# The gate product of an encoder layer by Strassen's seven products, with low parts and norm sums moved to POOL

## The chip, the cores and the metric

The kernel runs on one core of one Trainium2 chip. The metric is the device time of one execution in microseconds (us). The engines are called as the profile calls them: PE (matrix products; PEld is its weight load), DVE (vector), ACT (activations and scaled copies), POOL (the general-purpose engine, which also issues DMAs that add into their target) and SP (the queue that issues plain DMAs). Each engine takes its instructions in order, from a queue of its own; semaphores tie the queues together.

## The reference

The reference is one layer of a causal encoder on 1024 positions of width 1024, in float32. Ahead of what is changed here come a pooling mixer, chunked attention, an output projection and a gated MLP of width 2816, whose last product adds into the residual `h`. The change concerns what follows:

```python
hn = rmsnorm(h, norm_ple_g[i])
gate = jax.nn.sigmoid(hn @ w_ple_gate[i] + b_ple_gate[i])   # 1024 x 1024 x 1024
h = h + gate * (p[i] @ w_ple[i])                            # 1024 x 256 x 1024
return rmsnorm(h, final_g)
```

## The kernel before

Everything is kept transposed: `H[d]` (d = 0 to 7) holds 128 features of the residual on the partitions, and the 1024 positions in the free dimension, in two halves `HS[0]` and `HS[1]` of 512. Float32 products are made of three matmuls (`mm3`, lines 135 to 137): each operand is split into a high part, rounded by a copy on ACT (line 140), and a low part, the rest, subtracted on DVE (line 141); the three are high by high, high by low, low by high. They add up in PSUM, whose eight banks of 128 x 512 are `PS[:, 0]` to `PS[:, 7]`.

The body of the kernel (the MLP) is the same before and after. The end of the kernel, which is rebuilt, has these stages, in the order in which PE takes them (PE's order is that of the code; the orders of DVE, ACT, POOL and SP are set by a scheduler, from priorities in the order of the code and its own estimate of when things are ready):

- *PLE product, first half* (`ple_mm(0, d, ...)`): `p @ w_ple` for positions 0 to 511, 8 tiles of 6 matmuls, copied by ACT to `po` (line 1314).
- *Last down tiles, first half* (`down_mm(d, 0, ...)`): the last two of the MLP's 22 row blocks, 8 tiles of 6 matmuls; DVE adds each into `H[d]` (line 1071). Between them stand the 8 tiles of the PLE product's second half.
- *Last down tiles, second half* (`down_mm(d, 1, ...)`): 8 tiles again.
- *Gate product*: 8 output tiles for the first half (`gate_mm`), 8 for the second, of which the last three are cut into 256 positions each. A tile of 512 positions takes 8 x 3 matmuls. The weights `w_gate` come in 8 loads of 512 KB, are split on ACT and DVE, and stay resident.
- After each tile `gate_out` (lines 1348 to 1352): multiply by the norm's factors in `rst2` (first half only; for the second half the operand was normed beforehand, `normed2`), sigmoid on ACT, times `po`, added to `H[d]`.
- *End*: the last norm, transposes on PE (`turn`), a scaled copy, and the store.

A norm (class `Norm`) has these steps: ACT squares each `H[d]` (lines 809, 811), DVE adds the squares (line 813), PE sums over the partitions (`sums`, line 819), DVE scales the sums (line 822), POOL raises them to the power -1/2 (line 823), PE spreads the result over the partitions (`rows`, line 827), ACT copies it out (line 829). `norm_a` and `norm_b` are the two halves' norms ahead of the gate; `last` are those of the end, whose `emit` (line 1367) multiplies the finished `H` and stores it. `sums` and `rows` are on PE's in-order queue: for `norm_a` they stood after the first and after the second gate tile.

Of the kernel before, what the change touches and what calls it, by code (L numbers as in the profile page):

```python
# [6 lines left out]
F32 = mybir.dt.float32  # L7
# [4 lines left out]
P = 128  # L12
SEQ = 1024
# [87 lines left out]
def trunk(tc, xT, pT, vecs, w_qk0, w_in, w_v, bias, counts, pool_w, w_out, w_up, w_down,  # L101
# [4 lines left out]
    with tc.tile_pool(name="sb", bufs=1) as sb, \  # L106
# [5 lines left out]
        R = sb.tile([P, 32768], F32R, name="R")  # L112
# [3 lines left out]

        b_pool = tc.tile_pool(name="b1", bufs=1)
# [4 lines left out]
        def r(kb, n):  # L122
            if kb >= 128:
                return B[:, int((kb - 128) * KW):int((kb - 128) * KW) + n]
            return R[:, int(kb * KW):int(kb * KW) + n]

# [31 lines left out]
        xh = [r(32 * h, 8192) for h in range(2)]  # L158
        XTH = [a[:, 0:4096].rearrange("p (k t) -> p k t", k=KT) for a in xh]
        XTL = [a[:, 4096:8192].rearrange("p (k t) -> p k t", k=KT) for a in xh]  # L160
        V = r(64, 8192).rearrange("p (k h c) -> p k h c", k=NTOK, h=N_HEADS)
# [104 lines left out]
        def v_outs(t, half, ps):  # L266
# [3 lines left out]
            hi, lo = V[:, t, hs, 0:HD], V[:, t, hs, HD:2 * HD]  # L270
# [172 lines left out]
        def values(u):  # L443
# [23 lines left out]
            for j in range(2):  # L467
                for n_, (part, k) in enumerate(todo):
                    a, b = reach[k]
                    b0 = block_at(k, a)  # L470
                    pe.matmul(Os[j][:, (a - t0) * P:(b - t0) * P].rearrange("p (t q) -> p t q", q=P), V[:, k, 2 * c_ + j],  # L471
# [799 lines left out]
        b_pool.__exit__(None, None, None)  # L1271
        b_pool = tc.tile_pool(name="po", bufs=1)
        PO = b_pool.__enter__().tile([P, 7168], F32, name="PO")
        po = [PO[:, 512 * n:512 * (n + 1)] for n in range(14)] + [V[:, 0:512], V[:, 512:1024]]
        for d in range(4):
# [3 lines left out]
        wg = [(r(b, 1024), r(b + 4, 1024)) for b in (16, 24, 80, 88, 44, 52)] + [(r(b, 1024), r(b + 8, 1024)) for b in (96, 112)]  # L1279
        hp = [[(r(b, 512), r(b + 2, 512)) for b in bs]  # L1280
              for bs in ((100, 108, 116, 124, 32, 36, 40, 60), (0, 4, 8, 12, 64, 68, 72, 76))]
        rawg = [f(44, 1024), f(48, 1024), f(52.25, 1024)]
        ng = [0]

        def gate_weights(ks):
            for k in ks:
                t = rawg[ng[0] % 3]
                ng[0] += 1
                sp.dma_start(t, w_gate[k])
                split(t, *wg[k])  # L1290

        rst2 = f(48.25, SEQ)
        norm_a = Norm(HS[0], f(56.25, 512), [f(58.25, 512)], 5, 1)
        norm_b = Norm(HS[1], f(52.25, 512), [f(54.25, 512)], 4, 1)

        def weighted2(h, k, src=None):
            hi, lo = hp[h][k]
            src, g = H[k][:, HS[h]] if src is None else src, vec[:, C_GP + k:C_GP + k + 1]
            act.activation(hi, src, AF.Copy, scale=g)
            dve.scalar_tensor_tensor(lo, src, g, rv(hi), ALU.mult, ALU.subtract)  # L1300

        def normed2(k):

            t = f(44 + 2 * (k % 2), 512)
            dve.tensor_tensor(t, H[k][:, HS[1]], rst2[:, HS[1]], ALU.mult)
            weighted2(1, k, t)

        ple_banks = (0, 1, 2, 4, 5, 6, 7, 3)
# [6 lines left out]

        for d in range(KT):
# [9 lines left out]
        for k in range(KT):  # L1326
            weighted2(0, k)
        gate_weights(range(4, 8))
# [178 lines left out]
```

## Time and profile before

| | |
|---|---|
| median of 3 runs | 1124.37 us (1124.28 to 1124.96) |
| profiled execution, its own time | 1124.14 us |
| its span, first to last instruction | 1122.3 us (1.8 us lie around it) |
| mean granted PE clock | 0.998 |
| PE busy in the end stages, 976.6 to 1113.0 us of the span | all of it |
| busy from 1020.2 to 1113.0 us (the gate) | PE 92.8, DVE 58.2, ACT 43.6, POOL 4.3 us |
| from the gate's last matmul to the end | 9.3 us |

The page gives each engine's busy time; a busy PE counts overlapping matmuls once, so the distance between two matmuls' starts says what one costs. In a row of the timeline stand start, duration, engine, line, operation and tiles, and in brackets the idle time before it and what ended that. A group row of the lines view has busy time and mean duration (ns) of one instruction.

### The profile page before, as it was taken

The numbers are of one execution on the slowest core, as the hardware profiler recorded it, in microseconds if no ns is written. First come the engines' busy times: TensorE is split into PE (matmuls) and PEld (weight loads), VectorE is DVE, ScalarE is ACT, GpSimd is POOL, SyncE is SP. The second block draws the span as 40 slices with busy tenths as digits, with TensorE's granted clock in tenths as the row PEclk, the third lists the DMA queues.
The fourth block names the chain that finished last, engine by engine and source line by source line (L and its number), as shares of the span: only waits on it lengthen the run. The fifth ranks groups of instructions, "written<-read, shape, count | busy, mean of one in ns | idle before, by whom it ended". The sixth has DMA issues, their size and how long they took to land.

```text
span 1122.3 us, 16025 instructions
## 1 busy us (share of the span) xinstructions
PE 1112.2 (99%) x5866; PEld 932.0 (83%) x5866; DVE 853.5 (76%) x1442; ACT 583.7 (52%) x1010; POOL 166.7 (15%) x212
## 2 busy tenths in 40 slices
PE   9999999999999999999999999999999999999997
PEld 7978799888888888888888888888888888888887
DVE  7466676678668878878787878787877789986845
ACT  8366676665664544444443435343444444664634
POOL 0012000186003200210122011201120112000000
PEclk9999999999999999999999999999999999999999
DMA  8101020204610352674667455756575556430003
GB/s 282 38 20 62 20 63 19 61 19 132 196 35 5 99 161 87 159 170 133 159 152 171 138 160 142 175 144 155 144 170 151 132 154 132 147 94 20 1 26 124
DMA packets 64591, 124.86 MB, mean 111 GB/s; under 512 B 7296, under 2 KB 8704, under 8 KB 64512
## 3 DMA queue, kind: packets, MB, share of 16 engines
q1 hardware_dynamic: 50400, 98.33, 27.0%
q0 software_dynamic: 13824, 25.17, 14.0%
q8 instruction: 46, 0.75, 0.3%
q10 hardware_dynamic: 288, 0.33, 0.1%
q14 instruction: 33, 0.27, 0.1%
HBM read 109.13 MB, written 14.68 MB: 110 GB/s over the span
## 4 chain that ended last, share of the span: by engine, by line
PE 89%; DVE 4%; issue 3%; ACT 2%; POOL 1%; DMA 0%; POOLq 0%; SPq 0%; DVEq 0%; ACTq 0%
PE PS L135 28%; PE PS L136 28%; PE PS L137 27%; PE PS L471 2%; PE PS L396 2%; PE PS L419 1%; DVE R L141 1%; DVE B L439 1%; ACT F L376 1%; ACT R L140 1%; DMA F<-in_xT 0%; POOL TB L966 0%; PE PS L819 0%; DVE F L948 0%; DVE F L1232 0%
## 5 line engine op out<-in xcount | busy, mean ns | idle before, releaser
L135 PE MATMUL PS<-R 128*128 128x512 f32 (+1 forms) x1152 | 441.2, 383 | 0.1
L137 PE MATMUL PS<-R 128*128 128x512 f32 (+1 forms) x1152 | 437.2, 380 | 0.0
L136 PE MATMUL PS<-R 128*128 128x512 f32 (+1 forms) x1088 | 419.3, 385 | 0.3 <-DVE R L245 0.3
L135 PEld LDWEIGHTS PS<-R 128*128 128x128 f32 x1152 | 216.9, 188 | 45.0 <-issue 2.5
L137 PEld LDWEIGHTS PS<-R 128*128 128x128 f32 x1152 | 216.8, 188 | 40.9
L136 PEld LDWEIGHTS PS<-R 128*128 128x128 f32 x1088 | 204.7, 188 | 40.5 <-DVE R L245 1.1
L140 ACT ACTIVATE R<-F 128x512 fp32r<-128x512 f32 (+2 forms) x221 | 137.3, 636 | 176.4 <-PE PS L136 77.1
L141 DVE TENSOR_TENSOR R<-F,R 128x512 fp32r<-128x512 f32 (+2 forms) x221 | 154.2, 712 | 49.3 <-ACT R L140 48.8
L891 DVE TENSOR_TENSOR F<-F 128x512 f32<-128x512 f32 x88 | 60.5, 688 | 49.5 <-DMA F<-in_w_up 45.9
L1201 DVE TENSOR_TENSOR F<-F,PS 128x512 f32<-128x512 f32 x140 | 92.5, 682 | 5.9 <-PE PS L137 5.8
L140 ACT ACTIVATE BQ<-RW 128x512 fp32r<-128x512 f32 x90 | 52.6, 622 | 78.6 <-PE PS L136 74.6
L1144 POOL DMA_DIRECT2D RW<-Yd x56 | 49.2, 879 | 266.9 <-DMA RW<-Yd 202.8
L1144 POOL DMA_DIRECT2D RW<-in_w_down x40 | 36.1, 951 | 225.0 <-DMA RW<-in_w_down 190.6
L141 DVE TENSOR_TENSOR BQ<-RW,BQ 128x512 fp32r<-128x512 f32 x90 | 59.1, 686 | 1.8 <-PE PS L136 1.3
L136 PE MATMUL PS<-BQ 128*128 128x512 f32 x140 | 54.7, 390 | 0.1
L137 PE MATMUL PS<-R,BQ 128*128 128x512 f32 x140 | 54.6, 390 | 0.0
L135 PE MATMUL PS<-R,BQ 128*128 128x512 f32 x140 | 54.6, 390 | 0.0
L135 PE MATMUL PS<-BQ 128*128 128x512 f32 x140 | 54.5, 389 | 0.0
L137 PE MATMUL PS<-BQ 128*128 128x512 f32 x140 | 54.5, 389 | 0.0
L136 PE MATMUL PS<-R,BQ 128*128 128x512 f32 x140 | 54.5, 389 | 0.0
L376 ACT ACTIVATE F<-F,small 128x640 f32<-128x640 f32 (+4 forms) x64 | 44.0, 689 | 18.5 <-DVE small L364 15.5
L1027 ACT ACTIVATE F<-F,vec 128x1024 f32<-128x1024 f32 (+1 forms) x25 | 28.6, 1143 | 47.3 <-DVE F L1002 42.5
(178 smaller groups left out, 1605.4 us busy)
## 6 DMA issues: line engine op xcount, KB each, us to landing
F<-in_w_up SPq DMA_DIRECT2D x91, 256.0 KB, 4.3
RW<-Yd SPq DMA_DIRECT2D x60, 256.0 KB, 3.9
RW<-Yd POOLq DMA_DIRECT2D x56, 256.0 KB, 5.0
RW<-in_w_down SPq DMA_DIRECT2D x50, 256.0 KB, 2.9
RW<-in_w_down POOLq DMA_DIRECT2D x40, 256.0 KB, 6.3
Yd<-F SPq DMA_DIRECT2D x40, 256.0 KB, 2.8
F<-in_w_in SPq DMA_DIRECT2D x10, 512.0 KB, 3.5
F<-in_xT SPq DMA_DIRECT2D x16, 256.0 KB, 5.7
```

Source lines behind the costliest of these rows:

```text
L135: pe.matmul(ps, ahi, bhi, start=first, stop=False, skip_group_check=more)
L136: pe.matmul(ps, ahi, blo, start=False, stop=False, skip_group_check=more)
L137: pe.matmul(ps, alo, bhi, start=False, stop=last, skip_group_check=more)
L140: both = (act.activation(hi, src, AF.Copy), dve.tensor_tensor(lo, src, rv(hi), ALU.subtract))
L141: dve.tensor_tensor(lo, src, rv(hi), ALU.subtract))
L376: push(1.9 + 0.85 * z, lambda S=S, s_=s_: act.activation(S, S, AF.Exp, bias=s_[:, 0:1], scale=-1.0, accum_out=s_[:, 1:2]))
L396: pe.matmul(PS[:, places[x][y], 0:wide], q[halves[x], t * P:(t + 1) * P], k[halves[x], ki + y * wide:ki + (y + 1) * wide], start=i == 0, s ...
L471: pe.matmul(Os[j][:, (a - t0) * P:(b - t0) * P].rearrange("p (t q) -> p t q", q=P), V[:, k, 2 * c_ + j], PT[part][:, b0:b0 + by * (b - a - ...
L891: return dve.tensor_tensor(rawu[to], rawu[a], rawu[b], op)
L1027: act.activation(y, Gb[:, 2 + a:2 + b], AF.Identity, bias=vec[:, C_CB + fi:C_CB + fi + 1], scale=cw(2))
L1144: pool.dma_start(t, src, accum_op=ALU.add)
L1201: dve.tensor_tensor(t, t, PS[:, 4 + d], ALU.subtract if n in (1, 5) else ALU.add)
```

## The change

- The gate product becomes a 2 x 2 block product by seven products instead of eight (a Strassen-like scheme with reused sums). The output's 8 feature tiles make four pairs (p, p + 4). For each pair there are seven products `n` of 4 x 3 matmuls of 512 positions (`gproduct`), 28 in all in the order `gorder`; the last three (n = 3 for p = 1, 2, 3) are cut into two halves of 256 positions. PSUM is seeded with earlier products by ACT copies (line 1475).
- The right-hand operands are seven sets of four split tiles (`form`), sums of gain-weighted halves of `H`. Sets 1 and 2 are made as the first half of the down tiles ends; sets 6, 4, 7 and 5 (lines 1401 to 1411: weighted copies on ACT, differences on DVE, `t7[k]` differences on POOL) while the second half's tiles come, and set 3 after that.
- The left-hand operands (sums of weight blocks) are made per product: a first load by SP, further blocks added by POOL's DMAs (20 of them), then split: high part on ACT (line 1346), low part on POOL (line 1347), into a ring of four, each four products ahead.
- All norms' factors now multiply the product (`gate_out`, line 1421), in the second half too.
- The squares' sums of `norm_a`, `norm_b` and the first of the last norms go to POOL (`add(d, pool)`, line 815). In `norm_a` and `norm_b` there is one buffer for the square.
- The PLE product's second half stands wholly ahead of the first half's down tiles.
- `norm_a.sums` stands after product 1 of 28, `norm_a.rows` after product 2; `norm_b.sums` after product 8, its `rows` after product 9. At the end the last two-quarter norm is applied after the last matmul (`emit(last[1])`), no longer in its midst.
- SBUF tiles are laid out anew (`R` gives 8192 words to `R2`, whose place `PO` takes later); the values `V` become one view per tile. The order of all engines ahead of the end stages is the same as before.

```diff
+        gorder = [(p, n) for n in (1, 2) for p in range(4)]
+        for q in (0, 2):
+            gorder += [(p, n) for n in (6, 7, 4, 5) for p in (q, q + 1)]
+            gorder += [(p, 3) for p in ((0,) if q == 0 else (1, 2, 3))]
...
+                for z, (o, half) in enumerate(gsource[n]):
+                    src = w_gate[p + o, :, half * 512:(half + 1) * 512]
+                    if z or n == 3:
+                        pool.dma_start(t, src, accum_op=ALU.add)
+                    else:
+                        sp.dma_start(t, src)
...
+        def gprepare(upto, eng=pool):
...
+                    act.activation(hi, src, AF.Copy)
+                    eng.tensor_tensor(lo, src, rv(hi), ALU.subtract)
...
+        def gproduct(bank, first, ts=slice(0, 512), more=False):
+            p, n = gorder[gdone[0]]
+            hi, lo = WG[gdone[0] % 4]
+            for k in range(4):
+                bh, bl = GF[n][k]
+                mm3(PS[:, bank, ts], hi[:, k], lo[:, k], bh[:, ts], bl[:, ts], first and k == 0, k == 3,
+                    not first)
...
+        def form(n, k, src, scale=None):
+            hi, lo = GF[n][k]
+            if scale is None:
+                split(src, hi, lo)
+            else:
+                act.activation(hi, src, AF.Copy, scale=scale)
+                dve.scalar_tensor_tensor(lo, src, scale, rv(hi), ALU.mult, ALU.subtract)
...
         for d in range(KT):
             ple_mm(0, d, ple_banks[d])
-        gate_weights(range(4))
+        gprepare(4, dve)
+        for d in range(KT):
+            ple_mm(1, d, ple_banks[d])
         for d in range(KT):
             down_mm(d, 0, banks[d], wd2, gv2)
             down_add(d, 0, banks[d])
-            norm_a.add(d)
-            ple_mm(1, d, banks[(d + 4) % 8])
+            norm_a.add(d, pool)
+            form(1 if d < 4 else 2, d % 4, H[d][:, HS[0]], gain(d))
...
-        for d in range(KT):
-            down_mm(d, 1, banks[d], wd2, gv2)
-            down_add(d, 1, banks[d])
-        for d in range(KT):
-            norm_b.add(d)
+        for z, d in enumerate((0, 4, 1, 5, 2, 6, 3, 7)):
+            down_mm(d, 1, banks[z], wd2, gv2)
+            down_add(d, 1, banks[z])
+            norm_b.add(d, pool)
+            if d > 3:
+                k, s = d - 4, d % 2
+                act.activation(b22, H[d][:, HS[1]], AF.Copy, scale=gain(d))
+                dve.scalar_tensor_tensor(t7[k], H[k][:, HS[1]], gain(k), b22, ALU.mult, ALU.subtract)
+                dve.scalar_tensor_tensor(t6[s], H[k][:, HS[0]], gain(k), t7[k], ALU.mult, ALU.subtract)
+                form(6, k, t6[s])
+                dve.scalar_tensor_tensor(t4, H[d][:, HS[0]], gain(d), t6[s], ALU.mult, ALU.subtract)
+                form(4, k, t4)
+        for k in range(4):
+            form(7, k, t7[k])
+        for k in range(4):
+            pool.tensor_tensor(t7[k], H[k][:, HS[0]], H[k][:, HS[1]], ALU.subtract)
+            form(5, k, t7[k], gain(k))
...
+        after = {(0, 1): norm_a.sums, (1, 1): lambda: norm_a.rows(rst2[:, HS[0]]), (3, 2): norm_b.sums,
+                 (0, 6): lambda: norm_b.rows(rst2[:, HS[1]]),
...
+        ends = [(p, h) for h in range(2) for p in (1, 2, 3)]
...
+            gproduct(BZ[p], False, ts, True)
+            a = 512 + h * 256
+            gate_out(p, a, a + 256, spare(), PS[:, BZ[p], ts])
+            last[1 + h].add(p)
...
+        last[1].rows()
+        emit(last[1])
```

Three places show how instructions now stand on the engines. Line numbers in rows of the kernel before are those of the profile; after the change `Norm`'s lines stand two lower (822 is 824, 823 is 825).

On DVE, around the scaling of `norm_a`'s sums (L822): before, it stands behind the last adds of squares (L813), ahead of the first `gate_out` (L1348).

```order
L1071 TENSOR_TENSOR F<-F,PS 128x512
L813 TENSOR_TENSOR F<-F 128x512 x4
L822 TENSOR_SCALAR small<-PS 128x4
L1348 TENSOR_TENSOR F<-PS,F 128x512 x2
L1351 TENSOR_TENSOR F<-PO,F 128x512 x2
```

Now (L824) it stands behind the low parts of sets 6, 4 and 7 (L145), the differences that feed them (L1402, L1403, L1405), and the four low parts of set 5 (the first L1374):

```order
L1402 SCALAR_TENSOR_TENSOR F<-F,vec 128x512
L145 TENSOR_TENSOR R<-F,R 128x512
L1403 SCALAR_TENSOR_TENSOR F<-F,vec 128x512
L145 TENSOR_TENSOR R<-F,R 128x512
L1405 SCALAR_TENSOR_TENSOR F<-F,vec 128x512
L145 TENSOR_TENSOR R<-F,R 128x512 x4
L1374 SCALAR_TENSOR_TENSOR R<-F,vec,R 128x512 x4
L824 TENSOR_SCALAR small<-PS 128x4
```

The small instruction for which PE's `rows` wait has moved behind all of the operands' making.

On POOL before, after the MLP's last accumulating DMAs (L1144), only the norms' small powers are left:

```order
L1144 DMA RW<-in_w_down 128x512 x2
L823 TENSOR_TENSOR small<-small 128x4 x3
L823 TENSOR_TENSOR small<-small 128x2
L1442 TENSOR_TENSOR small<-small 128x2
L1502 UNCONDITIONAL_BRANCH
```

Now, ahead of `norm_a`'s power (L825), POOL has the adds of squares (L815), accumulating weight DMAs (L1332), two low parts of weights (L1347) and the `t7` differences (L1410). These are the last twelve rows up to that power; ahead of them stand eight L815, an L1332, an L815 and an L1332.

```order
L815 TENSOR_TENSOR F<-F 128x512 x3
L1347 TENSOR_TENSOR R<-F,R 128x512
L815 TENSOR_TENSOR F<-F 128x512
L1332 DMA F<-in_w_gate 128x512
L1410 TENSOR_TENSOR F<-F 128x512
L815 TENSOR_TENSOR F<-F 128x512
L1347 TENSOR_TENSOR R<-F,R 128x512
L1332 DMA F<-in_w_gate 128x512
L1410 TENSOR_TENSOR F<-F 128x512
L1332 DMA F<-in_w_gate 128x512
L1410 TENSOR_TENSOR F<-F 128x512 x2
L825 TENSOR_TENSOR small<-small 128x4
```

POOL, which had one instruction to do here, now has a queue in front of it.

On DVE at the kernel's end, before: the work of the last two half tiles (L1351, L1352, L813), with the emit of the third quarter (L1367) between.

```order
L813 TENSOR_TENSOR F<-F 128x256
L1367 TENSOR_TENSOR F<-F,PS 128x4x256 x2
L1351 TENSOR_TENSOR F<-V,F 128x256
L1352 TENSOR_TENSOR F<-F 128x256
L813 TENSOR_TENSOR F<-F 128x256
L1351 TENSOR_TENSOR F<-V,F 128x256
L1352 TENSOR_TENSOR F<-F 128x256
L1441 TENSOR_SCALAR small<-PS 128x2
```

Now both emits (L1435, of `last[0]` and of `last[1]`) are mixed with the six half tiles; these are the last twelve rows up to the last add into `H` (L1424), which stands behind them:

```order
L1435 TENSOR_TENSOR F<-F,PS 128x2x512 x3
L1421 TENSOR_TENSOR F<-PS,F 128x256 x2
L824 TENSOR_SCALAR small<-PS 128x2
L1423 TENSOR_TENSOR F<-PO,F 128x256 x2
L1424 TENSOR_TENSOR F<-F 128x256 x2
L1421 TENSOR_TENSOR GK<-PS,F 128x256
L815 TENSOR_TENSOR GK<-GK 128x256
L1435 TENSOR_TENSOR F<-F,PS 128x4x256
L815 TENSOR_TENSOR GK<-GK 128x256
L1423 TENSOR_TENSOR GK<-PO,GK 128x256
L1435 TENSOR_TENSOR F<-F,PS 128x4x256
L1424 TENSOR_TENSOR F<-F,GK 128x256
```

DVE's work between the last full product and the last add has grown from what two half tiles need to six half tiles, two rests of full ones and six emits.

More of the change, by code (lines that the diff above doesn't have):

```diff
@@ L1283, in trunk @@
[L1283 to L1290, printed above, removed]
-        rst2 = f(48.25, SEQ)
[L1293 to L1300, printed above, removed]
@@ L1402, in trunk, with first_half, second_half @@
-        gate_banks = (7, 2, 3)
-        for i, (g, d, a, b) in enumerate(units):
-            gate_mm(d, a, b, gate_banks[i % 3], scaled if (g, d) == (2, whole + 1) else None)
-            if i == 0:
-                norm_a.sums()
-                continue
+            last[1].n = last[2].n = n + 1
+        def first_half(d, bank):
+            gate_out(d, 0, 512, spare(), PS[:, bank])
+            last[0].add(d, pool)
+            final_g(d, HS[0])
+        def second_half(d, t, ps=None):
+            gate_out(d, 512, 1024, t, ps)
+            add_both(d)
+            final_g(d, HS[1])
@@ new lines, in trunk @@
+        g_pool = tc.tile_pool(name="gk", bufs=1)
+        GK = g_pool.__enter__().tile([P, 8192], F32, name="GK")
+        gk = [GK[:, 512 * n:512 * (n + 1)] for n in range(16)]
+        grown += gk[0:2]
+        zt += gk[8:10]
+        kept_u, kept_p, squares, square = gk[2:4], gk[4:6], gk[6], gk[7]
+        last += [Norm(slice(512, 768), squares[:, 0:256], [square[:, 0:256]], 1, 1),
+                 Norm(slice(768, 1024), squares[:, 256:512], [square[:, 256:512]], 1, 1, False)]
+        run_to((1, 3))
```

215 lines of the change are left out of this document (136 added, 79 removed).

## The prediction

> **What bounds the kernel now.** I read the page's busy times, then the chain of work that ended last, then the windows of the two end stages.
>
> ```profile
> PE 1112.2 (99%) x5866; PEld 932.0 (83%) x5866; DVE 853.5 (76%) x1442; ACT 583.7 (52%) x1010; POOL 166.7 (15%) x212
> PE 89%; DVE 4%; issue 3%; ACT 2%; POOL 1%; DMA 0%; POOLq 0%; SPq 0%; DVEq 0%; ACTq 0%
> 1020.20:1113.00 92.80, 92.80 (x499) 80.27 (x498) 58.19 (x94) 43.55 (x70) 4.33 (x4) 1.00 0.07 27
> ```
>
> PE never rests, and the chain that ended last is 89% PE. The window row (length; then busy time of PE, its weight load, DVE, ACT, POOL; clock; DMA share; GB/s) is the gate: PE full, DVE with 34.6 us to spare, POOL nearly unused. So a matmul less there is time won, as long as PE still finds its operands. The kernel's last part, behind PE, is read from these rows:
>
> ```profile
> 1112.92 0.29 PE L137 MATMUL PS<-R 128*128 128x256 f32 x1
> 1113.75 0.43 DVE L1351 TENSOR_TENSOR F<-V,F 128x256 f32<-128x256 f32 x1
> 1114.21 0.42 DVE L1352 TENSOR_TENSOR F<-F 128x256 f32<-128x256 f32 x1
> ```
>
> The last add into `H` (L1352) ends at 1114.63, 1.4 us after PE's last product. From it to the span's end at 1122.3 the same chain (square, sums, power, copy, store) runs before and after. So I ask only when the last add ends. What is late there is late at the end.
>
> **The matmuls removed.**
>
> ```profile
> 1093.77 0.39 PE L135 MATMUL PS<-R 128*128 128x512 f32 x1
> 1095.13 0.28 PE L135 MATMUL PS<-R 128*128 128x256 f32 x1
> 1106.52 0.28 PE L137 MATMUL PS<-R 128*128 128x256 f32 x1
> 1025.59 0.95 PE L819 MATMUL PS<-small,F 128*128 128x1 f32 x8
> 1026.40 0.49 PE L135 MATMUL PS<-R 128*128 128x512 f32 x1
> 1031.98 0.60 PE L827 MATMUL PS<-ident,small 128*128 128x128 f32 x4
> 1032.34 0.48 PE L135 MATMUL PS<-R 128*128 128x512 f32 x1
> ```
>
> Six full matmuls lie between the first two rows: (1095.13 - 1093.77)/6 = 0.2267 us each; 95 half ones between the second and third: 0.1199. Before, the gate has 312 full and 144 half matmuls, 70.7 + 17.3 = 88.0 us; after, 25 products of 12 full and 6 of 12 half, 68.0 + 8.6 = 76.6. On PE alone 11.4 us go. `sums` takes 0.81 (next two rows), `rows` 0.36. The gate starts 24 matmuls ahead of `sums`, at 1025.59 - 5.44 = 1020.15, the second half's down tiles 48 ahead of that, at 1009.27, the first half's 96 ahead, at 998.39.
>
> **The new wait of PE.** After product 2, at 1020.15 + 5.44 + 0.81 = 1026.4, PE meets `norm_a.rows`, and all later products are queued behind it. Before, this wait ended here:
>
> ```profile
> 1028.13 0.16 DVE L822 TENSOR_SCALAR small<-PS 128x4 f32<-128x4 f32 x1
> 1028.38 1.03 POOL L823 TENSOR_TENSOR small<-small 128x4 f32<-128x4 f32 x1 [76.54 <-DVE small L822]
> ```
>
> Before, POOL had idled 76.5 us for it, and the power was done 2.6 us ahead of PE. Now the power stands behind 14 adds of squares, 4 differences, 2 low parts and 5 accumulating DMAs on POOL; the scaling stands on DVE behind the low parts of set 5, which need those differences. The prices:
>
> ```profile
> L956 POOL TENSOR_TENSOR F<-TB 128x512 f32<-128x512 f32 x4 | 5.6, 1402 | 5.3 <-ACT TB L937 5.3
> L966 POOL TENSOR_TENSOR TB<-TB 128x512 f32<-128x512 f32 x4 | 7.8, 1958 | 28.8 <-DVE TB L960 18.9 <-DVE R L141 9.8
> L500 POOL TENSOR_TENSOR R<-F,R 128x512 fp32r<-128x512 f32 x7 | 9.4, 1342 | 56.4 <-ACT R L502 56.4
> L1144 POOL DMA_DIRECT2D RW<-in_w_down x40 | 36.1, 951 | 225.0 <-DMA RW<-in_w_down 190.6 <-DVE BQ L141 18.9 <-DVE R L141 13.3
> L811 ACT ACTIVATE F<-F 128x512 f32<-128x512 f32 x14 | 8.8, 630 | 12.5 <-DVE F L1352 6.7 <-DVE F L813 5.8
> L1299 ACT ACTIVATE R<-F,vec 128x512 fp32r<-128x512 f32 x8 | 5.5, 715 | 1.2 <-DVE F L1305 1.0
> RW<-Yd POOLq DMA_DIRECT2D x56, 256.0 KB, 5.0
> F<-in_pT SPq DMA_DIRECT2D x4, 256.0 KB, 3.4
> ```
>
> No row has an add of squares on POOL. The bounds are 1.34 (a subtraction of the same size, L500) and 1.96 (L966, in DVE's busiest stretch). I take 1.40 (L956), since DVE will itself be waiting here half the time.
>
> POOL's first add needs two down tiles (2.72), a DVE add (0.6), a square (0.63) and handoffs (my estimate 0.36: 0.17 by which a half matmul's 0.29 outlasts its 0.12, and 0.06 to 0.12 from engine to engine): 1002.7. There is one buffer for the square, so each next add waits for the last add, then a square: a round is 1.40 + 0.63 + 0.12 = 2.15. Seven adds end at 1002.7 + 6 x 2.15 + 1.40 = 1017.0. `norm_b`'s first add needs a copy and two squares on ACT behind the last square: 1017.6 to 1019.0. Then the DMA for the square's buffer waits for SP's load, which could start only at 1017.0: 1020.4 (landing 3.4). One add follows. The next DMA adds into the same buffer and waits until the first has landed, 5.0 after 1020.4: 1025.4, done 1026.4. An add to 1027.8; a square, an add to 1030.0; three ACT copies and a square, then an add from 1031.3 to 1032.7; four ACT copies, the low part from 1034.1 to 1035.4; add 1036.8; DMA 1037.8; difference 1039.2; add 1040.6; low part 1041.9; DMA 1042.9; difference 1044.3; DMA, again held by an SP load (issued 1041.9, landed 1045.4), 1046.4; two differences 1049.2. Then ACT's high part 0.72, DVE's low part 0.66, the scaling 0.16, the power 1.03 and handoffs 0.3: 1052.1. PE waits 1052.1 - 1026.4 = **25.7 us**. In this list 10 adds and 3 differences are covered neither by ACT's copies nor by a landing; so at 1.34 it gives 13 x 0.06 = 0.8 less, 24.9, and at 1.96 13 x 0.56 = 7.3 more, 33.0.
>
> [...]
>
> **PE after the wait.** PE has no idle stretch in the middle of the kernel before. The nearest row is its start:
>
> ```profile
> 1.49 3.78 PE L220 MATMUL PS<-B 128*128 128x512 f32 x8 [1.49 <-DVE B L218]
> 5.16 0.70 PE L135 MATMUL PS<-R 128*128 128x512 f32 x1
> ```
>
> There eight matmuls take 3.67 us, against 8 x 0.2267 = 1.81. I charge 1.9 us; bounds 0 and 1.9. [...]
>
> **Smaller waits.** `norm_b`'s power stands on POOL behind a low part and a DMA that waits for an SP load: 1.9 us (bounds 0, and 4.35 - 2.72 = 1.6 more if the DMA starts a product later). Products 20 to 22 (third and fourth pair) take PSUM that ACT must first copy out, and on ACT these copies stand behind sigmoids and scaled copies that wait for DVE's rests of the first two pairs: some five steps of 0.6 to 0.7 against one product of 2.72, 4.1 us for the three (bounds 0 and 6). Together 6.0.
>
> **The end.** The last full product ends at E = 1020.15 + 68.0 + 2.3 (two `sums`, two `rows`) + 25.7 + 1.9 + 6.0 = 1124.1. The six half products (8.6 us) are then no longer the limit. DVE is:
>
> ```profile
> 1049.30 0.69 DVE L1305 TENSOR_TENSOR F<-F 128x512 f32<-128x512 f32 x1
> 1049.90 0.69 DVE L813 TENSOR_TENSOR F<-F 128x512 f32<-128x512 f32 x1
> 1051.10 0.75 DVE L1300 SCALAR_TENSOR_TENSOR R<-F,vec,R 128x512 fp32r<-128x512 f32 x1
> 1051.76 0.69 DVE L1305 TENSOR_TENSOR F<-F 128x512 f32<-128x512 f32 x1
> 1109.66 2.35 DVE L1367 TENSOR_TENSOR F<-F,PS 128x1024 f32<-128x1024 f32 x2 [0.51 <-PE PS L827]
> ```
>
> Starts lie 0.60 apart for a full instruction (0.66 for the three-operand one), 0.09 less than the 0.69 it lasts, so a half one costs 0.43 - 0.09 = 0.35; an emit step is (2.35 - 0.09)/2 = 1.13. After E: 0.8 until the product is read out, 9 full instructions of the two last full products (5.4), 23 half ones (8.05), 6 emit steps (6.8), scalings and waits 0.4: 21.5. The last add ends at 1145.6 instead of 1114.63: +30.9.
>
> **At no cost.** The PLE product's second half moves by whole tiles, 48 matmuls as before, its eight ACT copies under PE; if they came late PE would wait one tile, 1.4 us. The new layout of SBUF changes no instruction. SP's 24 loads and POOL's 20 DMAs move 11 MB instead of 4 in a stage with a DMA share of 0.07. ACT's and POOL's further work (POOL: 19 low parts, 15 DMAs, 7 adds, 50 us against 57 of the products) lies under PE. If POOL's cover goes (1.96 throughout) it is a match for PE: rival C.
>
> **Sum**, against the profiled execution's own 1124.14 us (span 1122.3 and 1.8 around it; 0.23 below the median of the runs): 1124.14 + 30.9 = **1155.0**.
>
> **The rivals.**
> - *B: POOL's list is short, and only DVE's queue holds PE.* From 1010.8 (first read-out of the second half's tiles) DVE has 20 instructions at 0.60 and 17 at 0.66, 23.2 us, and 1.3 of waits, then 1.3 for scaling and power: 1036.6, a stall of 10.2; the end would be 1155.0 - 15.5 = 1139.5. It asks for rounds of half the price, against every POOL row.
> - *C: POOL at 1.96.* Stall 33.0, time 1162.3; with weights late some us more.
> - *D, the other side: the wait at `rows` is covered.* If the power were ready by 1026.4, as it was before, and the smaller waits with it, E is 1090.5, the last add 1112.0, the time 1121.5, 2.6 us faster. It decides below 2.6 us of waits in all. For it speaks only that PE's products 3 to 8 need neither set 5 nor the norm; against it, that PE's queue is in order.
> - *E: no smaller waits, cold PE free:* 1155.0 - 7.9 = 1147.
>
> That the change does not cut products is ruled out by the counts.
>
> **How the numbers follow.** The forecast 0.70 (own range 1149 to 1160: landing of DMAs a us earlier or later at four places, handoffs, prices 1.34 to 1.60), C 0.12, E 0.08, B 0.05, D 0.03, and 0.02 within 0.2% (2.2 us), which is about what a measurement of this kernel can tell from no change. The range 1144 to 1164 leaves out B, D and C's upper end. Faster by over 0.2% is D alone; slower is the rest.
>
> **What would show it.** Right: PE idle for some 25 us after product 2, ended by POOL's power (L825); products at 2.72 us after it; matmuls at about 0.45 for the first eight; POOL's adds near 1.4 and ACT's squares waiting for them; DVE back to back for 21 us from the last full product to the last L1424. Wrong: an idle stretch under 15 us (the adds are cheaper, or scheduled otherwise than I follow them), a stretch over 31 (contention), or a tail in which PE still sets the end.

## The result, and the profile after

| | before | after |
|---|---|---|
| median of 4 runs each | 1124.32 us (1124.03 to 1124.96) | 1163.9 us (1162.63 to 1164.5) |
| profiled execution: its span | 1122.3 us | 1162.7 us |
| mean granted PE clock | 0.998 | 0.979 |

The change makes the kernel slower: 1.035 times the time before, 95% interval 1.0332 to 1.0368, or +39.6 us. The forecast was +30.9, a time of 1155.0. The measured 1163.9 lies outside the forecast's own range (1149 to 1160) and at the upper edge of the wide one (1144 to 1164).

The page of the changed kernel, its engines' busy times and the chain that ended last:

```profile
PE 1112.1 (96%) x5782; PEld 927.8 (80%) x5782; DVE 879.1 (76%) x1452; ACT 609.4 (52%) x1062; POOL 254.6 (22%) x281
PE 4%; DVE 3%; issue 1%; ACT 1%; POOL 0%; DVEq 0%; POOLq 0%; ACTq 0%
```

PE has 84 instructions fewer and the same busy time, since some of those that are left run slowly (below), and it is now idle for 4% of the span. The chain can be followed back only a short way, through the end stages. There it alternates between PE and DVE; before, 89% of it was PE.

What PE waited for from 1000 us to the end (total, times, longest; before, no wait stands here up to its last product):

```profile
PE PS L829 <- POOL small L825: 33.7, 3, 26.3
PE PS L139 <- DVE PS L1475: 4.2, 1, 4.2
```

And PE's own rows at the three waits ahead of the last full product, and at the one behind it (start, duration, ..., idle time and its releaser in brackets):

```profile
1054.15 1.11 PE L829 MATMUL PS<-ident,small 128*128 128x128 f32 x4 [26.28 <-POOL small L825]
...
1078.95 0.79 PE L829 MATMUL PS<-ident,small 128*128 128x128 f32 x4 [1.91 <-POOL small L825]
...
1104.51 0.79 PE L139 MATMUL PS<-R 128*128 128x512 f32 x1 [4.21 <-DVE PS L1475]
...
1142.56 1.11 PE L829 MATMUL PS<-ident,small 128*128 128x128 f32 x4 [5.48 <-POOL small L825]
```

PE idles 26.28 us at `norm_a.rows`, until POOL's power (L825). The windows view shows who was busy meanwhile (length; then busy time of PE, its weight load, DVE, ACT, POOL; clock; DMA share; GB/s):

```profile
1026.50:1054.00 27.50, 1.38 (x6) 0.78 (x5) 27.42 (x30) 15.42 (x26) 21.15 (x15) 0.59 0.38 83
```

DVE is busy for 27.42 of 27.5 us, POOL for 21.15. DVE's groups in the wait (1027 to 1054 us) show what filled it:

```profile
L145 DVE TENSOR_TENSOR R<-F,R 128x512 fp32r<-128x512 f32 x11 | 14.5, 1335 | 0.1
...
L1073 DVE TENSOR_TENSOR F<-F,PS 128x512 f32<-128x512 f32 x3 | 2.0, 674 | 0.0
```

A low part (L145), priced at 0.60 to 0.69 us, now takes 1.335 us on the mean, while a read-out with one operand in PSUM (L1073) takes 0.674, as before. The last rows of the two queues ahead of PE's release:

```profile
1048.74 3.73 DVE L1374 SCALAR_TENSOR_TENSOR R<-F,vec,R 128x512 fp32r<-128x512 f32 x4
1052.39 0.15 DVE L824 TENSOR_SCALAR small<-PS 128x4 f32<-128x4 f32 x1
1048.96 1.64 POOL L1410 TENSOR_TENSOR F<-F 128x512 f32<-128x512 f32 x1 [0.69 <-DVE R L145]
1052.62 1.48 POOL L825 TENSOR_TENSOR small<-small 128x4 f32<-128x4 f32 x1 [2.02 <-DVE small L824]
```

POOL itself waits 2.02 us for DVE's scaling (L824), which stands behind four low parts of set 5, whose last operand POOL's difference (L1410) had delivered. So the two queues hold each other, and PE waits for both.

After each of the first three waits PE runs slowly. The matmuls behind the first, and the first at full pace:

```profile
1055.92 0.63 PE L141 MATMUL PS<-G,R 128*128 128x512 f32 x1
1056.35 0.63 PE L139 MATMUL PS<-G,R 128*128 128x512 f32 x1
...
1059.12 0.40 PE L140 MATMUL PS<-G,R 128*128 128x512 f32 x1
1059.35 0.40 PE L141 MATMUL PS<-G,R 128*128 128x512 f32 x1
```

They start 0.43 us apart at first, 0.23 at the end. The granted clock is 0.50 from 1054.92 to 1058.48 us and 1.00 from 1058.88 to 1062.00. Against 0.2267 each, 9 matmuls cost 1.92 us more here, 8 cost 1.65 after the second wait, and 13 cost 2.69 after the third.

The end, read as before: the first half matmul (E, where the last full product has ended), and the last add into `H` (L1424):

```profile
1131.73 0.28 PE L139 MATMUL PS<-R 128*128 128x256 f32 x1
1154.59 0.41 DVE L1424 TENSOR_TENSOR F<-F,GK 128x256 f32<-128x256 f32 x1
```

E lies at 1131.73 us, the last add ends at 1155.0, 40.4 us later than before. From there to the span's end it is 7.7 us, as before.

### The profile page after: what moved, and what is told of

Same layout as the page of the kernel before. It is cut to its first block, busy times and chain, and to the rows that moved or that the text cites. A ratio compares the mean times of both kernels' runs of the same rounds, so it can differ in the third digit from the quotient of the medians.

```text
span 1162.7 us, 16098 instructions
## 1 busy us (share of the span) xinstructions
PE 1112.1 (96%) x5782; PEld 927.8 (80%) x5782; DVE 879.1 (76%) x1452; ACT 609.4 (52%) x1062; POOL 254.6 (22%) x281
## 5 line engine op out<-in xcount | busy, mean ns | idle before, releaser
L139 PE MATMUL PS<-R 128*128 128x512 f32 (+1 forms) x852 | 329.3, 387 | 4.5 <-DVE PS L1475 4.2
L141 PE MATMUL PS<-R 128*128 128x512 f32 (+1 forms) x820 | 315.7, 385 | 0.0
L140 PE MATMUL PS<-R 128*128 128x512 f32 (+1 forms) x724 | 281.6, 389 | 0.0
L144 ACT ACTIVATE R<-F 128x512 fp32r<-128x512 f32 (+1 forms) x225 | 135.8, 620 | 169.4 <-PE PS L140 80.6
L139 PEld LDWEIGHTS PS<-R 128*128 128x128 f32 x852 | 162.5, 191 | 39.5 <-DVE PS L1475 4.6
L145 DVE TENSOR_TENSOR R<-F,R 128x512 fp32r<-128x512 f32 (+1 forms) x225 | 159.4, 724 | 43.3 <-ACT R L144 41.8
L141 PEld LDWEIGHTS PS<-R 128*128 128x128 f32 x820 | 156.2, 190 | 30.7
L140 PEld LDWEIGHTS PS<-R 128*128 128x128 f32 x724 | 138.1, 191 | 27.4
L140 PE MATMUL PS<-R,R 128*128 128x512 f32 x304 | 119.0, 392 | 0.0
L141 PE MATMUL PS<-R,R 128*128 128x512 f32 (+1 forms) x272 | 102.6, 377 | 0.1
L139 PE MATMUL PS<-R,R 128*128 128x512 f32 x240 | 93.7, 390 | 0.1
L144 ACT ACTIVATE BQ<-RW 128x512 fp32r<-128x512 f32 x90 | 52.6, 622 | 75.7 <-PE PS L140 71.7
L140 PEld LDWEIGHTS PS<-R,R 128*128 128x128 f32 x304 | 57.3, 189 | 11.4 <-DVE R L247 0.2
L145 DVE TENSOR_TENSOR BQ<-RW,BQ 128x512 fp32r<-128x512 f32 x90 | 59.0, 683 | 1.1 <-ACT BQ L144 0.5
L141 PEld LDWEIGHTS PS<-R,R 128*128 128x128 f32 x272 | 51.2, 188 | 10.0 <-DVE R L145 0.5
L140 PE MATMUL PS<-BQ 128*128 128x512 f32 x140 | 54.7, 391 | 0.1
L141 PE MATMUL PS<-BQ 128*128 128x512 f32 x140 | 54.5, 389 | 0.0
```

The lines of the kernel that those rows point to most:

```text
L139: pe.matmul(ps, ahi, bhi, start=first, stop=False, skip_group_check=more)
L140: pe.matmul(ps, ahi, blo, start=False, stop=False, skip_group_check=more)
L141: pe.matmul(ps, alo, bhi, start=False, stop=last, skip_group_check=more)
L144: both = (act.activation(hi, src, AF.Copy), dve.tensor_tensor(lo, src, rv(hi), ALU.subtract))
L145: dve.tensor_tensor(lo, src, rv(hi), ALU.subtract))
```

## The experiments

Times are single runs beside the kernel before (1124.10 or 1124.12 us on the same chips) unless an interval is given; the kernel as changed has 1163.9. "Slow matmuls" are full ones more than 0.33 us apart.

**e1: keep PE busy through the wait.** 110 matmuls that nobody reads stand ahead of `norm_a.rows`.

```diff
-(1, 1): lambda: norm_a.rows(rst2[:, HS[0]])
+(1, 1): lambda: [[pe.matmul(PS[:, 6], ...) for _ in range(110)], norm_a.rows(rst2[:, HS[0]])]
```

> 110 full matmuls that nothing reads (25 us) fill PE's wait ahead of the first norm's rows; nothing else changes. If the slow matmuls behind each wait come from PE's idling, the first eight after the wait start 0.23 us apart instead of 0.43, the wait's end stays at 1054 us of the span, and the span falls by 1.9 us to 1160.8. If they come from their operands or from DVE's load, the 0.43 stays and so does the span, 1162.7.

Measured 1166.44 us. The matmuls did not fill the wait: 2.77 us of idling were left, and 8 slow matmuls followed (9 without them). This run says nothing on their cost, only that they came behind 2.77 us of idling too.

**e2: leave out POOL's adds of squares.** The 21 adds that the change gave to POOL are not computed (the norms are then those of a single tile's square).

```diff
-                    if self.n < KT - 1 or self.whole:
+                    if eng is not pool and (self.n < KT - 1 or self.whole):
```

> Leaves out the adds of squares on POOL (21: seven each for the two norms ahead of the gate and for the first of the last norms), so the norms are of the last squares only. Theory A (POOL's list holds the power): ten of the fourteen adds in the list are not covered by anything, at 1.3 to 1.7 us with the squares' rounds between them, so the wait at the first rows falls from 26.3 to about 16 us and the span from 1162.7 to about 1150. Theory B (DVE's forming of the operands holds it; DVE was busy 27.4 of the 27.5 us of the wait): the wait stays within 2 us, the span at 1161 to 1163.

Measured 1149.94 us, with this wait at the rows:

```profile
1044.13 1.11 PE L829 MATMUL PS<-ident,small 128*128 128x128 f32 x4 [17.30 <-POOL small L825]
```

The wait falls by 9.0 us, the time by 14.0. POOL's list is a large part of the wait, but 17.3 us of it are left without the adds.

**e3: the sums and rows of `norm_a` early in the scheduler's order.**

```diff
-after = {(0, 1): norm_a.sums, (1, 1): lambda: norm_a.rows(rst2[:, HS[0]]), ...
+after = {(0, 1): lambda: soon(norm_a.sums, 300), (1, 1): lambda: soon(lambda: norm_a.rows(rst2[:, HS[0]]), 300), ...
```

> The first norm's scaling (DVE), power (POOL) and rows' copy (ACT) get a higher priority, so that they stand ahead of the differences and low parts on each engine; no work changes. If only their place in the queues costs time (theory A alone), the 26.3 us of waiting and 1.9 us of slow matmuls go: span 1135. If the operands' making is itself as long as the wait (theory B), PE waits again one to seven products later, for the operands: span 1155 to 1162. My sum from the durations seen lies between: about 9 us of wait left at the rows, 8 to 9 us in later waits, span 1152.

Measured 1156.87 us. The first wait shrinks, but others take its place:

```profile
PE PS L829 <- POOL small L825: 12.6, 2, 6.3
PE PS L139 <- ACT GK L1475: 6.4, 1, 6.4
PE PS L821 <- DVE F L1421: 5.6, 1, 5.6
PE PS L139 <- ACT F L831: 4.9, 1, 4.9
```

Ahead of the last full product, the waits at the rows, the copy of the factors (L831), the next norm's sums (L821) and a seed (L1475) sum to 6.3 + 4.9 + 5.6 + 6.4 = 23.2 us, against 32.4 in the kernel as changed. Of 20 us saved at the rows 9 stay saved. The expectation's own sum had too little left in the later waits: 8 to 9 us, where 16.9 were left. The order of the scaling is not the whole cause: what stood ahead of it is now late for something else.

**e4: the adds of squares of `norm_a` and `norm_b` back on DVE.**

```diff
-            norm_a.add(d, pool)
+            norm_a.add(d)
...
-            norm_b.add(d, pool)
+            norm_b.add(d)
```

> The adds of squares of the two norms ahead of the gate go back to DVE (14 of 0.60 us). Theory A: POOL's list is shorter by its adds, DVE's longer by 8.4 us, of which part lies under waits: wait 26.3 down to about 21, span 1157. Theory B: DVE's list is what counts, so the wait grows by up to 8.4 us: span 1165 to 1171.

Measured 1162.93 us, the wait 24.7 us, so neither theory's number came out (21, or more than 26.3). Putting the fourteen adds on DVE wins 1.6 us of the 9.0 that leaving them out wins: DVE's queue is full in this stretch (27.42 of 27.5 us above), so what POOL gives up there lengthens DVE's.

**e5: e1 with 124 matmuls.**

```diff
-for _ in range(110)
+for _ in range(124)
```

> As e1, but with 124 full matmuls (28 us): in e1 PE still stood idle for 2.8 us behind the 110, and the next eight matmuls were 0.43 us apart again. Now the idle rest is under 0.5 us. If PE's slowness comes from idling, all matmuls after the rows are 0.23 us apart, and the stage behind the wait is 1.9 us shorter than in e1 (or in the changed kernel, when its wait ends at the same time). If two or three us of idling don't matter and something else slows them, they stay at 0.43.

Measured 1163.64 us. Now PE is busy until the power is there, and the timeline at the rows reads:

```profile
1055.57 0.60 PE L829 MATMUL PS<-ident,small 128*128 128x128 f32 x4
1055.92 0.48 PE L139 MATMUL PS<-G,R 128*128 128x512 f32 x1
1056.24 0.39 PE L140 MATMUL PS<-G,R 128*128 128x512 f32 x1
1056.47 0.39 PE L141 MATMUL PS<-G,R 128*128 128x512 f32 x1
```

Right behind the rows matmuls come 0.32 and then 0.23 us apart. So at this place it is the idling that makes them slow. Little is gained: the extra matmuls end the wait later (first product at 1055.92 instead of 1054.92), E lies at 1129.97, 1.8 us earlier than without them.

**e6: leave out the emits' multiplications** (six instructions of 1024 columns on DVE; `H` is stored without its last scaling).

```diff
-                dve.tensor_tensor(h_, h_, norm.out.unsqueeze(1).to_broadcast([P, n, norm.nt * P]), ALU.mult)
```

> Leaves out the emits' multiplications on DVE (six of 1.13 us; the stores go out without the last norm's factor). If DVE sets the end (my prediction), the time from the last full product to the last add into H, 23.3 us in the changed kernel, falls by 6.8 to about 16.5, and the span to 1156. If PE's own 5.5 us wait for the last norms' rows sets it, or the chain through ACT, under 2 us are won: span 1161 to 1163.

Measured 1161.21 us. E lies at 1130.77 and the last add ends at 1151.70: a tail of 20.9 us instead of 23.3. Of 7.1 us of work left out, the tail loses 2.4. DVE waits for PE instead:

```profile
1146.16 0.42 DVE L1421 TENSOR_TENSOR F<-PS,F 128x256 f32<-128x256 f32 x1 [1.86 <-PE PS L141]
1149.60 0.42 DVE L1421 TENSOR_TENSOR GK<-PS,F 128x256 f32<-128x256 f32 x1 [0.21 <-PE PS L141]
```

PE has its own wait in the tail (at the rows of the first of the last norms, 6.31 us in this run), with three half products queued behind it, which end at 1149.6. That wait is itself made by DVE's list: the scaling (L824) that it needs starts there at 1141.12, while PE's sums had begun at 1133.65. DVE's list and PE's in-order queue both hold the end.

**e7: adds, low parts and differences all on DVE.** POOL keeps the powers and its DMAs.

```diff
-        def gprepare(upto, eng=pool):
+        def gprepare(upto, eng=dve):
...
-            norm_a.add(d, pool)
+            norm_a.add(d)
...
-            pool.tensor_tensor(t7[k], H[k][:, HS[0]], H[k][:, HS[1]], ALU.subtract)
+            dve.tensor_tensor(t7[k], H[k][:, HS[0]], H[k][:, HS[1]], ALU.subtract)
```

(and likewise `norm_b.add` and `last[0].add`)

> Takes back one part of the change, the work moved to POOL: all adds of squares (21), the low parts of the weights (24) and the differences of set 5 (4) are done on DVE; POOL keeps its DMAs and powers. If offloading relieves DVE, DVE has 49 x 0.60 = 29 us more in the gate and the span grows, by 5 to 15 us, to 1168 to 1178. If POOL's instructions slow DVE's by about as much as they take off it (DVE's L145 took 1.34 us in the wait, beside POOL, against 0.68 elsewhere), DVE's instructions fall back to 0.68, the wait at the rows to about 22 us, and the span is the same or shorter: 1155 to 1163.

Measured 1155.97 us, 7.9 us faster than with POOL's help. The wait at the rows is 21.4 us. DVE's low parts in the same window as above:

```profile
L145 DVE TENSOR_TENSOR R<-F,R 128x512 fp32r<-128x512 f32 x10 | 6.7, 686 | 1.1 <-ACT R L144 1.1
L1374 DVE SCALAR_TENSOR_TENSOR R<-F,vec,R 128x512 fp32r<-128x512 f32 x8 | 5.5, 747 | 0.0
```

With POOL nearly quiet a low part takes 686 ns, half of the 1335 beside POOL. Over the end stages, from 976 us to each span's end, the windows are these (this run first, then the kernel as changed):

```profile
976.00:1154.20 178.20, 137.69 (x637) 115.36 (x635) 128.62 (x214) 103.22 (x178) 22.75 (x25) 0.89 0.37 86
976.00:1162.70 186.70, 140.16 (x639) 116.41 (x637) 127.12 (x166) 104.21 (x179) 91.00 (x74) 0.87 0.34 82
```

DVE is busy for 128.6 us and POOL for 22.8; in the kernel as changed for 127.1 and 91.0. So 68 us of POOL's time bought DVE 1.5 us.

**e8 and e10: e7 in a better order.** `norm_a`'s sums and rows early as in e3; `norm_b`'s squares after the operands, its sums after product 11 and rows after product 12; the weights' splits at another priority; product (1, 3) moved ahead, so that two products are halved at the end, not three; the first norm's sums earlier, and half of its emit on POOL.

```diff
+        with tc.high_priority(20):
+            for d in (0, 4, 1, 5, 2, 6, 3, 7):
+                norm_b.add(d, dve)
...
+                 ... (0, 7): lambda: soon(norm_b.sums), (1, 7): lambda: soon(lambda: norm_b.rows(rst2[:, HS[1]])),
...
-        ends = [(p, h) for h in range(2) for p in (1, 2, 3)]
+        ends = [(p, h) for h in range(2) for p in (2, 3)]
...
+                emit(last[0], pool, rst2[:, HS[0]], range(0, 2))
```

> The same seven products with the other steps arranged anew: everything but DMAs and powers off POOL as in e7 (half of the first half's emit goes to POOL, where it is alone); the first norm ahead in priority as in e3; the second norm's squares behind the operands, its sums after product 10 and rows after product 11; product 3 of pair 1 taken ahead of the second two pairs, so that two products are cut in halves instead of three; the last norms' sums straight after their squares. From the durations: about 7 us of waits of PE in the gate, the last add into H some 25 us sooner than in the changed kernel: span about 1132, between the two kernels. If the seven products cost DVE and ACT more than any order can hide, it stays above 1150; if only order was wrong, it falls below the kernel before, 1122.

Measured 1136.51 us, 27 us faster than the kernel as changed. Which of these steps won how much was not taken apart. The same kernel again, in four runs:

> The kernel of e8 again (adds, low parts and differences on DVE, sums and rows early, two products halved instead of three), timed in rounds beside the kernel before, to have an interval for it: one look gave 1136.5 against 1124.1. Theory (DVE's and ACT's further work, 129 us of DVE instead of 100 from 976 to 1150, keeps it behind the kernel before): a ratio of 1.009 to 1.013. Rival (the look was an outlier, and the matmuls saved show once PE's long wait is gone): a ratio at or below 1.002.

Measured 1136.79 us against 1124.18, a ratio of 1.0111 (1.0094 to 1.0128). PE's waits are small now:

```profile
PE PS L139 <- DVE GK L1423: 4.8, 1, 4.8
PE PS L139 <- ACT F L831: 3.8, 1, 3.8
PE PS L829 <- POOL small L825: 3.5, 2, 2.4
PE PS L821 <- DVE F L1423: 1.3, 1, 1.3
```

With two more of 0.8 us each they still sum to 15.0 us, more than the 11.4 us of matmuls saved, and slow matmuls behind two of them cost 4.0 more. Less the 11.4 that makes 7.6 of the 12.6 us lost; the other 5 were not traced. What the other engines do is in the windows of the two kernels, 976 to 1150 us (both spans end before that; before first):

```profile
976.00:1150.00 174.00, 140.11 (x718) 119.50 (x716) 99.79 (x155) 77.65 (x125) 5.03 (x5) 0.98 0.13 46
```

```profile
976.00:1150.00 174.00, 136.35 (x619) 112.91 (x617) 128.17 (x206) 101.19 (x173) 27.74 (x27) 0.92 0.37 88
```

By the counts the seven products give PE 11.4 us less to do, and DVE is busy for 28.4 us more and ACT for 23.5. That this work makes the waits is argued from these rows; no run takes it away. No version that was run is faster than the kernel before.

**e9: one part of the change alone, in the kernel before.** The 14 adds of `norm_a` and `norm_b` go to POOL; products and weights stay as they were.

```diff
-            norm_a.add(d)
+            norm_a.add(d, pool)
...
-            norm_b.add(d)
+            norm_b.add(d, pool)
```

> The kernel before with one part of the change alone: the 14 adds of squares of the two last norms stand on POOL instead of DVE; products, weights and low parts as before. Theory (POOL and DVE slow each other, and this costs time only where DVE or POOL has no slack): DVE's low parts beside these adds, which read two tiles of SBUF (L1300, mean 749 ns before; L141 of 1024 columns, 1223 ns before), last on the mean 1.3 to 1.9 times as long, the read-outs with one PSUM source (L1071, 680 ns) stay within 5%; the last add of squares ends near 1030, so the power still comes before PE reaches the rows at 1031.6, PE doesn't wait, and the time is the same within 0.3% (1121 to 1128). Rival 1 (the longer DVE rows of the change come from its own operands or buffers, not from POOL): L1300 and L141 stay within 5% of 749 and 1223. Rival 2 (POOL's order alone makes PE's wait, without the seven products): the power comes 1 to 4 us late behind the 14 adds in rounds of 2.03, PE waits at the rows and then runs slowly for some 8 matmuls: 1127 to 1131.

Measured 1129.28 us against 1124.18, a ratio of 1.0045 (1.003 to 1.006): 5.1 us slower. DVE's groups from 998 to 1030 us, here and then in the kernel before:

```profile
L1071 DVE TENSOR_TENSOR F<-F,PS 128x512 f32<-128x512 f32 x13 | 8.5, 676 | 0.0
L1300 DVE SCALAR_TENSOR_TENSOR R<-F,vec,R 128x512 fp32r<-128x512 f32 x6 | 7.3, 1211 | 5.0 <-ACT R L1299 4.9
L141 DVE TENSOR_TENSOR R<-F,R 128x1024 fp32r<-128x1024 f32 x4 | 4.9, 1218 | 2.4 <-ACT R L140 2.4
```

```profile
L1300 DVE SCALAR_TENSOR_TENSOR R<-F,vec,R 128x512 fp32r<-128x512 f32 x6 | 4.5, 750 | 0.4 <-ACT R L1299 0.4
```

The six L1300 go from 750 to 1211 ns. The read-outs from PSUM (L1071) keep their price. So do the four L141, though they too read two tiles of SBUF, where the expectation had them slower. The pairs of rows that overlap in time say why (POOL and DVE in this run):

```profile
1005.04 1.30 POOL L813 TENSOR_TENSOR F<-F 128x512 f32<-128x512 f32 x1 [1.95 <-ACT F L811]
1005.62 1.28 DVE L1300 SCALAR_TENSOR_TENSOR R<-F,vec,R 128x512 fp32r<-128x512 f32 x1 [1.37 <-ACT R L1299]
...
1020.97 1.22 DVE L141 TENSOR_TENSOR R<-F,R 128x1024 fp32r<-128x1024 f32 x1 [1.22 <-ACT R L140]
1021.53 1.82 POOL L813 TENSOR_TENSOR F<-F 128x512 f32<-128x512 f32 x1 [5.26 <-ACT F L811]
```

Where POOL's add began first, it keeps its 1.30 us and DVE's instruction ends at 1006.90, 0.56 us behind the add's end. Where DVE's began first, it keeps its 1.22 us and POOL's add takes 1.82, to 1023.35, 1.16 behind DVE's end. In both pairs the later one is held by the earlier one (alone it takes 0.75 or 1.29 us). So the contention shows with nothing else changed, and the first rival falls. Most of the lost time came as the second rival said: the adds run in rounds of 2.03 us, the last ends at 1035.50 (5.5 us later than expected), and PE waits at the rows:

```profile
1034.24 1.26 POOL L813 TENSOR_TENSOR F<-F 128x512 f32<-128x512 f32 x1 [0.74 <-ACT F L811]
1035.46 1.03 POOL L823 TENSOR_TENSOR small<-small 128x4 f32<-128x4 f32 x1
1036.55 0.65 PE L827 MATMUL PS<-ident,small 128*128 128x128 f32 x4 [2.37 <-POOL small L823]
1036.96 0.47 PE L135 MATMUL PS<-R 128*128 128x512 f32 x1
1037.27 0.39 PE L136 MATMUL PS<-R 128*128 128x512 f32 x1
```

`norm_a`'s power stands behind `norm_b`'s adds. No slow matmuls follow this wait. Of the 4.6 us by which this profiled span (1126.9) is longer than before, these 2.37 are half; 0.79 are a wait of PE for ACT's copy of the PLE product (L1314) at 1015 us, and 0.9 were there before the end stages began.

## Why the prediction was right, and what it mis-sized

**The direction and the main mechanism** were right: PE's queue is in order, `norm_a.rows` stands in it after product 2, and its power comes from POOL behind operands that are made by POOL and DVE. The matmuls saved are real, and worth less than the wait.

**The sum to E.** Forecast 1124.1, measured 1131.73:

| term | forecast, us | measured, us | off by |
|---|---|---|---|
| gate starts | 1020.15 | 1021.32 | +1.2 |
| wait at `norm_a.rows` | 25.7 | 26.28 | +0.6 |
| smaller waits | 6.0 | 1.91 + 4.21 = 6.12 | +0.1 |
| slow PE | 1.9 | 1.92 + 1.65 + 2.69 = 6.3 | +4.4 |
| 25 products, sums, rows | 70.3 | 71.7, the rest | +1.4 |

- *Slow PE* is the term that was mis-sized. The step charged it once, behind the long wait, and at that place 1.9 was right to the tenth. But it is paid after each of three waits, 6.3 us in all. e5 shows the idling to be the cause behind the first wait: without it the matmuls there come 0.32 and then 0.23 us apart.
- *The wait at the rows*: 25.7 against 26.28, and POOL's list carries much of it, as e2 shows (9 us of 26.3). But that the number came out so close is in part luck, with two errors in its working. POOL's adds were cheaper alone than priced (1.29 us instead of 1.40) and dearer beside DVE (1.41 to 1.72); and DVE, whose low parts were taken at their old price, was slowed to 1.335 us and was the last to finish. Rival B, a short POOL list and a wait of 10.2 us set by DVE's queue alone, fell short: without the adds 17.3 us were left (e2), and with POOL's part on a DVE at its old price 21.4 (e7). Rival C's time (1162.3) lies nearer to the measured one than the forecast's, but its mechanism did not run: its wait was to be 33.0 us, not 26.28, and no add of POOL's in this wait took more than 1.72, against its 1.96.
- *The smaller waits* were right in sum, the larger of them by luck. The one at `norm_b.rows` came as forecast (1.9, measured 1.91). The other 4.1 us were put at products 20 to 22, behind ACT's copies; these did not wait. Product 17 did, 4.21 us, for DVE's subtraction into its PSUM bank (L1475). On DVE that stands behind an add of two SBUF tiles (L1424), which took 4.77 us instead of 0.69, while POOL was at work without a gap (two DMA issues and two low parts of weights, 1094.23 to 1098.60 us):

```profile
1094.38 4.77 DVE L1424 TENSOR_TENSOR F<-F 128x512 f32<-128x512 f32 x1
1096.69 1.91 POOL L1347 TENSOR_TENSOR R<-GK,R 128x512 fp32r<-128x512 f32 x1
```

  In e7, without POOL's low parts, the three such adds (L1424) from 1120 to 1130 us take 0.69 us each and this wait is gone.
- *The start* of the gate was 1.2 us late. It does not come from the end stages: PE's 5000th matmul, well ahead of them, starts at 943.12 us instead of 941.95. Executions scatter here: e6, whose code is the same up to the gate, starts it at 1019.83.
- *The products*, 1.4 us: the slowly run spreading matmuls of the two `rows` (0.77 and 0.44 us instead of 0.36) are 0.5 of it; 0.5 is the last matmul ahead of each of three waits, which lasts 0.39 instead of the 0.23 of a step; 0.2 the longer step (0.32) behind each of two `sums`; and 0.2 the mean step of the others, 0.2276 instead of 0.2267.

**The tail** from E to the last add is 23.3 us instead of 21.5. The step "the six half products are then no longer the limit. DVE is" was half right. DVE is busy for 22.43 of these 23.3 us:

```profile
1131.70:1155.00 23.30, 15.88 (x109) 14.77 (x107) 22.43 (x42) 11.96 (x24) 3.30 (x4) 0.85 0.28 106
```

1.0 of the 1.8 us is again DVE's price beside POOL: the L1421 at 1131.90 us takes 1.73 (0.68 for the next one) behind an add of POOL's from 1131.79 to 1133.08. But e6, which takes 7.1 us of DVE's work away, wins 2.4, since PE's rows and half products then end last. Two limits lie some 2 us apart here, and only one was priced. E and the tail are 7.6 + 1.8 = 9.4 us off, which is the whole difference of the profiled executions (1155.0 forecast, 1164.5 measured: 9.5).

**"At no cost: POOL's further work lies under PE"** was wrong as a step. Its 68 us of further work (91.0 against e7's 22.8) slow DVE by nearly as much as they take off it (1.5 us less busy), and e7, without them, is 7.9 us faster. DVE's low parts, with two inputs in SBUF, took 1.335 us beside POOL in the wait and 0.686 in e7; its read-outs, with one input in PSUM, took 0.674 in the same wait. The kernel before had one stretch that leaned this way (338 to 376 us): beside POOL's L966, DVE's L141 took 853 ns on the mean where one with another source took 686:

```profile
L141 DVE TENSOR_TENSOR R<-TB,R 128x512 fp32r<-128x512 f32 x15 | 12.7, 853 | 0.6 <-ACT R L140 0.4
L141 DVE TENSOR_TENSOR R<-F,R 128x512 fp32r<-128x512 f32 x4 | 2.7, 686 | 3.9 <-ACT R L140 3.9
```

The prediction's sums have a dearer price on POOL's side alone (1.96 us); it belonged on DVE's as well.

**Rival D**, the wait covered, is what e10 comes nearest to: with the long wait gone, the kernel still loses 12.6 us. So in the best order that was run the saving is still lost in smaller waits (15.0 us). That DVE's and ACT's work on the operands makes them is likely by the busy times, and not shown.

## What to carry to other kernels

A product saved by sums of operands is paid on the engines that make the sums and their low parts (here 11.4 us less on PE, and in e10 28.4 us more on DVE and 23.5 on ACT); ask whether these have room in the very stretch where PE waits for them, not over the whole span. Work moved to POOL beside a busy DVE was not free here, though POOL had been idle: beside DVE instructions that read two SBUF tiles, price the pair at nearly its sum (here 1.29 + 0.55 us, where two such instructions on DVE's own queue cost 2 x 0.60). A small instruction for which PE's in-order queue waits (here a scaling and a power on four columns) belongs ahead of bulk work on its own queue: so placed, in e3, it made the wait at the rows 6.3 us instead of 26.28, though only 9 of these 20 us stayed saved. And a stall of PE can cost more than its length: here three of them lasted 32.4 us, and the slow matmuls behind them cost 6.3 more.

## What the runs showed of the hardware

- Where an elementwise instruction of POOL's and one of DVE's with two SBUF inputs overlapped, the one that began second was held. In e9 (995 to 1036 us) and in the kernel as changed (1000 to 1054 us), DVE's instruction that began second ended 0.54 to 0.56 us behind POOL's in all 23 such overlaps of single rows, and POOL's that began second ended 1.12 to 1.16 us behind DVE's in 11 of 12 (1.59 in one, at 1025.84 us, where DVE's next instruction, begun 0.05 us ahead of POOL's, was held too). Alone they take 0.69 to 0.75 and 1.29 us, so the second did little while the first ran, and a pair cost nearly its sum. Where POOL's instructions followed each other without a gap, its DMA issues among them, one DVE instruction was held to the end of the whole series, though it began ahead of some of them: the L1424 at 1094.38 us above took 4.77 us and ended 0.55 behind POOL's end. In the wait of the kernel as changed, with DVE busy for 27.42 and POOL for 21.15 of 27.5 us, their rows interlock:

```profile
1034.39 1.72 POOL L815 TENSOR_TENSOR F<-F 128x512 f32<-128x512 f32 x1
1034.91 1.75 DVE L145 TENSOR_TENSOR R<-F,R 128x512 fp32r<-128x512 f32 x1
```

  L145 ends at 1036.66, 0.55 us behind POOL's 1036.11. Read-outs with a PSUM operand (L1073) took 0.67 to 0.69 us beside POOL, against 0.680 (L1071) in the kernel before, where POOL was quiet. What makes the one wait for the other is not shown.
- Slow matmuls came behind short waits of PE too, but not behind all. Over these runs, waits of 2.77 us and more ahead of full products were followed by 5 to 13 slow matmuls, most of them 0.43 us apart; of those between 0.8 and 2.6 us some were (1.91 in the kernel as changed: 8 matmuls; 2.39 in e10: 5; 2.52 in e1: 5; 1.30 in e8: 8, some 0.8 us behind it, where a wait of 1.20 had ended 4 us ahead) and some were not (2.37 in e9, 2.47 in e2, 0.83 in e10). The granted clock goes with them: in the kernel as changed it is 0.50 behind the waits of 1.91 and 4.21 us as well (1079.30 to 1082.00 and 1104.50 to 1109.00 us) and 1.00 once the matmuls are 0.23 us apart again (1083.10 to 1090.00 and 1110.15 to 1113.00); in e9, behind the wait of 2.37, it is 1.00 (1036.70 to 1045.00). What decides which of the shorter waits are followed by slow matmuls is not shown.
